# Scratch memory of a two-layer block laid out by pairs of heads: half the loads per group of the RWKV scan, the keys' rows in two buffers

## The chip, the cores and the metric

The kernel runs on one core of one Trainium2 chip. The metric is the device time of one launch in microseconds (us), the median of several runs. A core has TensorE (PE for its matmuls, PEld for its weight loads), VectorE (DVE), ScalarE (ACT), GpSimd (POOL) and SyncE (SP), which issues nearly all DMAs here. Each engine runs its own instructions strictly in program order. A second name of an engine with a q (SPq, PEldq) is its sequencer, which issues and waits.

## The reference

Two layers over 1024 latent tokens (D = 1024) and 256 context tokens. The first mixes by pooling and a short convolution; the second runs a bidirectional RWKV-7 scan of 8 heads of width 64 beside a convolution branch, and projects both out. What the change touches is the scan and what feeds it:

```python
def wkv_scan(r, w, k, v, a, bb, s0, reverse):
    def step(s, inp):
        r_t, w_t, k_t, v_t, a_t, b_t = inp
        sa = jnp.einsum("bhvk,bhk->bhv", s, a_t)
        s = s * w_t[:, :, None, :] + sa[..., None] * b_t[:, :, None, :] + v_t[..., None] * k_t[:, :, None, :]
        return s, jnp.einsum("bhvk,bhk->bhv", s, r_t)
...
def rwkv_branch(...):
    kk = heads(k * k_k).astype(jnp.float32)
    kk = kk / jnp.maximum(jnp.sqrt(jnp.sum(kk * kk, axis=-1, keepdims=True)), 1e-12)
    for d in range(2):
        a = jax.nn.sigmoid(a0[d] + (ua @ a1[d]) @ a2[d])
        k_d = heads(k * (1.0 + (a - 1.0) * k_a)).astype(jnp.float32)
        s_fin, o = wkv_scan(r_h, heads(decay), k_d, v_h, -kk, kk * a_h, init, reverse=(d == 1))
```

So for each head and direction the scan needs rows `a` = -kk and `r` (queries), rows `b` = kk*a and `k` (keys), and the values `v`. The context is scanned first and its final state starts the scan of the tokens.

## The kernel before, in words

**Stages.** The first layer runs to about 600 us, `odd_in` (projections of the second layer, and the preparation of the scan's rows) to about 925 us, `scan` to the end. `odd_in` and `scan` are written as small generators. A planner, class `Lists`, runs them against a table of costs: `yield "P", 700` says that the code up to the next yield takes 700 ns of TensorE, `"S", 4800, 300` that it takes 4800 ns of SP's queue and that its data is there 300 ns later, `"R", "bk"` that a buffer of pool `bk` is needed. The planner's choice, made when the program is built, fixes the order of instructions on each engine; the chip then runs these orders and waits by semaphores alone. A changed cost or count of buffers (`RES`) therefore moves instructions on all engines.

**odd_in.** The 8 heads are 4 pairs j (128 partitions: two heads of 64), the 1280 tokens are 5 units u of 256 (u = 4 is the context). `prep(j, u)` makes for both directions d and the 4 chunks of 64 tokens the query rows `ar` (slot 0: a, made on VectorE at L1247 and L1248; slot 1: r, made on GpSimd at L1240) and the key rows `bk` (L1222, L1223, L1244), and stores them to scratch memory in DRAM: `store_ar` to `ARD`, `turned` to `BKD` and, transposed, to `BTD`, `values` the transposed values to `VTD` (L1289).

**scan.** There are 20 groups G: two pairs of heads at a time (j and j+1, index c), 5 units, half a unit f (two chunks per direction). For each group:
- `group(G)` loads the query rows `w` from `ARD` (L1498, 8 loads: direction, head of the pair, pair), the key rows `bk` from `BKD` (L1505, 2 loads), and multiplies them on TensorE into scores `sc` (L1522), first for pair j, then for j+1. `w` has 5 buffers, `bk` has one.
- `invert(G)` gathers blocks of the scores (`eb`), stores them to `ED` (L1571, 2 DMAs), reads them back spread over partitions as `Bc` (L1578, 2 loads), and GpSimd inverts 16x16 triangular blocks in 15 steps (L1420, L1421).
- `levels(G)` builds the inverse up to 64x64 on TensorE (L1616, L1624, L1635, L1651), after ScalarE has copied GpSimd's result into `Xe` (L1608).
- `chain()` carries the state through the group's two steps: TensorE L1741, L1746, L1765, VectorE and ScalarE between. It needs the values `sv` (`load_sv`, L1670, 8 loads from `VTD`) and `bkt` (L1682, 2 loads from `BTD`).
- Beside it run matmuls of the convolution branch (`project`, L1960) and then of the output projection (L2102, L2307), placed by the planner in the gaps, and the convolution itself on VectorE (L1981).

**DMAs.** SP issues them one after the other. Each one uses one of eight semaphores in turn (DMAHW0 to DMAHW7), and waits before it is issued for the DMA that used the same semaphore before it, that is the one eight places earlier.

Of the kernel before, what the change touches and what calls it, by code (L numbers as in the profile page):

```python
# [179 lines left out]
class Kern:  # L180
# [727 lines left out]
    def odd_in(self, es):  # L908
# [247 lines left out]
        def prep(j, u):  # L1156
# [65 lines left out]
            nc.vector.tensor_tensor(out=bk[:, 0, :, 0, :], in0=c4(ta[:, 0, :]), in1=fold(F, 0, 0), op=ALU.mult)  # L1222
# [8 lines left out]
            ar = sp.tile([128, 2, 2, 4, 64], F32, tag="ar", name="ar")  # L1231

            def ends():
# [3 lines left out]
                if u < 4:  # L1237
                    yield "E", ("shift", j, 2)
                    yield "G", 1230
                    nc.gpsimd.tensor_tensor(out=ar[:, :, 1], in0=c4(rT[:, z]).unsqueeze(1).to_broadcast([128, 2, 4, 64]), in1=folds(E), op=ALU.mult)  # L1240
# [6 lines left out]
            nc.vector.scalar_tensor_tensor(out=ar[:, 0, 0], in0=c4(kk2), scalar=-2.0, in1=fold(E, 0, -1), op0=ALU.mult, op1=ALU.mult)  # L1247
            nc.vector.scalar_tensor_tensor(out=ar[:, 1, 0, :, ::-1], in0=c4(kk2), scalar=-2.0, in1=fold(E, 1, 1), op0=ALU.mult, op1=ALU.mult)  # L1248
# [27 lines left out]
        def values(j, u, v):  # L1276
# [12 lines left out]
            nc.sync.dma_start(out=self.VTD[j, u].rearrange("f p v -> p f v"), in_=Vx)  # L1289
# [1133 lines left out]
```

## Time and profile before

| | |
|---|---|
| median of 3 runs | 1552.14 us (1549.43 to 1553.41) |
| the profiled execution | 1545.31 us, its span 1543.5 us |
| TensorE busy, weight loads busy | 1381.1 us (89%), 1084.7 us (70%) |
| VectorE, ScalarE, GpSimd busy | 993.9 us (64%), 637.0 us (41%), 671.9 us (44%) |
| mean granted TensorE clock | 0.951 |
| chain that ended last | TensorE 49%, VectorE 17%, DMA 11%, GpSimd 10% |
| DMA | 174374 packets, 232.32 MB, 151 GB/s mean |

In a row of groups the fields are: line, engine, operation, out<-in, shapes, count, then busy us and mean ns of one, then the idle time of the engine ahead of it and what ended it. A row of waits reads: who waited for whom, us in total, times, the longest. A row of windows gives the stretch, its length, the busy us (and instructions) of PE, PEld, DVE, ACT and POOL, the granted clock, the DMA engines' share and GB/s. A row of the time line gives start, us, engine, line, operation; SPq rows are the issuing of DMAs.

### The profile page before, as it was taken

What the parts mean: (1) busy time and instruction counts of PE and PEld (TensorE: products, weight loads), DVE (VectorE), ACT (ScalarE), POOL (GpSimd) and SP (SyncE); (2) the same over time, 40 slices, a digit from 0 to 9 for tenths busy, and PEclk for the clock granted to TensorE, in tenths of its full rate; (3) what the DMA queues carried; (4) which work ended last, traced back from release to release, by engine and by line L of the source; (5) the groups of instructions that cost most, each with busy time, mean ns of one, the idle gap of its engine ahead of it and who ended that gap; (6) DMA issues with size and microseconds to landing.
All of it is one profiled execution on the core that took longest, in us unless ns stands there. A gap on an engine that the chain in (4) does not pass through costs nothing.

```text
span 1543.5 us, 32203 instructions
## 1 busy us (share of the span) xinstructions
PE 1381.1 (89%) x12820; PEld 1084.7 (70%) x12820; DVE 993.9 (64%) x1681; ACT 637.0 (41%) x1257; POOL 671.9 (44%) x925
## 2 busy tenths in 40 slices
PE   6899999998999999899889878888998988886996
PEld 1578788887888778677667656676776666764775
DVE  3744464545822561279999964778688777788567
ACT  2551112122322552356556531344445643657534
POOL 1343535548455532135545421755557246406003
PEclk9899999999999999999999989899998998898999
DMA  7413433634253210537657775655655566774223
GB/s 266 152 66 123 169 131 129 213 137 162 70 174 124 67 65 33 147 99 218 199 169 226 224 253 150 159 141 150 168 141 151 165 157 173 218 225 127 86 86 109
DMA packets 174374, 232.32 MB, mean 151 GB/s; under 512 B 38832, under 2 KB 130352, under 8 KB 174096
## 3 DMA queue, kind: packets, MB, share of 16 engines
q1 hardware_dynamic: 172928, 228.69, 48.7%
q8 instruction: 101, 1.65, 0.5%
q10 hardware_dynamic: 1296, 1.57, 0.3%
q14 instruction: 49, 0.40, 0.1%
HBM read 164.93 MB, written 63.31 MB: 148 GB/s over the span
## 4 chain that ended last, share of the span: by engine, by line
PE 49%; DVE 17%; DMA 11%; POOL 10%; issue 6%; ACT 5%; SPq 2%; DVEq 0%; POOLq 0%; ACTq 0%
PE d L302 25%; PE d L2102 3%; PE d L1960 3%; PE d L1016 3%; DMA Bc<-ED 2%; POOL X L1421 2%; POOL tmp L1420 2%; DMA bk<-BKD 2%; PE sc L1522 2%; PE d L944 2%; DMA ad<-in_ada_e 1%; POOL wl L268 1%; PE pa L1741 1%; PE pr L458 1%; DVE Z L1090 1%
## 5 line engine op out<-in xcount | busy, mean ns | idle before, releaser
L302 PE MATMUL d<-sx,wh 128*128 128x512 f32 x1152 | 365.8, 399 | 2.4 <-DVE sx L528 1.3
L302 PEld LDWEIGHTS d<-sx,wh 128*128 128x128 f32 x1152 | 220.5, 192 | 54.2 <-POOL sx L398 1.8
L302 PE MATMUL d<-sx,wl 128*128 128x512 f32 x576 | 233.1, 405 | 12.3 <-POOL wl L268 9.1
L1420 POOL TENSOR_TENSOR tmp<-X,Bc 128x120 f32<-128x120 f32 (+2 forms) x300 | 120.0, 400 | 195.0 <-DMA Bc<-ED 172.6
L1016 PE MATMUL d<-sx,wh 128*128 128x512 f32 x512 | 162.8, 400 | 0.0
L268 POOL TENSOR_TENSOR wl<-wr,wh 128x1024 fp32r<-128x1024 f32 x37 | 98.8, 2671 | 139.4 <-ACT wh L267 139.4
L629 DVE SCALAR_TENSOR_TENSOR junk<-wra,cb 128x1024 bf16<-128x1024 f32 x56 | 108.3, 1934 | 75.5 <-DMA wra<-in_ada_o 51.0
L1960 PE MATMUL d<-sx,wh 128*128 128x512 f32 x384 | 139.3, 430 | 0.0
L302 PEld LDWEIGHTS d<-sx,wl 128*128 128x128 f32 x576 | 110.4, 192 | 38.7 <-POOL wl L268 10.1
L1421 POOL TENSOR_TENSOR X<-X,tmp 128x120 f32<-128x120 f32 (+2 forms) x300 | 124.8, 416 | 23.5
L1016 PEld LDWEIGHTS d<-sx,wh 128*128 128x128 f32 x512 | 98.6, 193 | 22.1 <-issue 2.7
L1016 PE MATMUL d<-sx,wl 128*128 128x512 f32 x256 | 112.9, 441 | 0.0
L302 PE MATMUL d<-sc,wh 128*128 128x256 f32 x576 | 104.1, 281 | 0.0
L1960 PE MATMUL d<-sx,wl 128*128 128x512 f32 x192 | 83.8, 437 | 9.8 <-DVE wl L1934 9.8
L1981 DVE SCALAR_TENSOR_TENSOR acc<-hc,vec,acc 128x960 f32<-128x960 f32 (+14 forms) x120 | 90.0, 774 | 1.1
L302 PEld LDWEIGHTS d<-sc,wh 128*128 128x128 f32 x576 | 88.8, 190 | 1.4
L267 ACT CAST wh<-wr 128x1024 fp32r<-128x1024 f32 x37 | 38.7, 1046 | 119.8 <-PE d L302 64.5
L1960 PEld LDWEIGHTS d<-sx,wh 128*128 128x128 f32 x384 | 74.5, 200 | 16.5 <-issue 0.2
L302 PE MATMUL d<-sc,wl 128*128 128x256 f32 x288 | 81.0, 281 | 0.0
L1522 PE MATMUL sc<-w,bk 64*128 64x128 f32 (+1 forms) x640 | 55.4, 311 | 20.4 <-issue 9.1
L1522 PEld LDWEIGHTS sc<-w,bk 64*128 64x128 f32 x640 | 46.8, 210 | 28.2 <-issue 25.2
L1536 DVE TENSOR_TENSOR w<-sc,cstb 64x256 f32<-64x256 f32 x80 | 33.8, 422 | 47.2 <-PE sc L1522 28.5
(381 smaller groups left out, 2880.6 us busy)
## 6 DMA issues: line engine op xcount, KB each, us to landing
wr<-in_in_o SPq DMA_DIRECT2D x32, 512.0 KB
wr<-in_in_e SPq DMA_DIRECT2D x24, 512.0 KB
wra<-in_ada_o SPq DMA_DIRECT2D x24, 512.0 KB
BKD<-bk SPq DMA_DIRECT2D x40, 256.0 KB
BTD<-X SPq DMA_DIRECT2D x20, 512.0 KB
bk<-BKD SPq DMA_DIRECT2D x40, 256.0 KB
Bc<-ED SPq DMA_DIRECT2D x20, 512.0 KB
bkt<-BTD SPq DMA_DIRECT2D x40, 256.0 KB
```

Source lines behind the costliest of these rows:

```text
L267: self.nc.scalar.copy(hi, raw)
L268: self.nc.gpsimd.tensor_tensor(out=lo, in0=raw, in1=hi.bitcast(F32), op=ALU.subtract)
L302: self.nc.tensor.matmul(ps[:, :n], lhsT=w[a][:, k, :], rhs=rhs(src, k, b, c0, n), start=(i == 0), stop=(i == len(seq) - 1))
L629: nc.vector.scalar_tensor_tensor(out=junk, in0=w, scalar=1.0, in1=cb[:, s, :], op0=ALU.mult, op1=ALU.mult, accum_out=dst[:, s:s + 1])
L1016: nc.tensor.matmul(ps, lhsT=w[a][:, k, :], rhs=rhs(s, k, b, c0, m), start=(q == 0), stop=(q == len(seq) - 1))
L1420: g.tensor_tensor(out=t, in0=X[:, :, j:j + 1].to_broadcast([128, 8, m]), in1=B[:, j, :, j + 1:16] if j < 8 else B2[:, j - 8, :, j - 7:8], ...
L1421: g.tensor_tensor(out=X[:, :, j + 1:16], in0=X[:, :, j + 1:16], in1=t, op=ALU.add)
L1522: nc.tensor.matmul(ps[h][:, d, i, h:h + 1] if ctx else ps[h][:, d, i], lhsT=bk[R[h], c, d, i], rhs=w[R[h], c, d, sl, i, :], start=True, st ...
L1536: nc.vector.tensor_tensor(out=w[o, c, :, 2 * h], in0=ps[h][o, :, :, h], in1=ma[o].unsqueeze(2).to_broadcast([64, 2, 2, 64]), op=ALU.mult)
L1960: nc.tensor.matmul(ps, lhsT=wt(a, k), rhs=rhs("x", k, b, c0, 512), start=(i == 0), stop=(i == len(seq) - 1))
L1981: nc.vector.scalar_tensor_tensor(out=acc[:, o], in0=hc[:, q], scalar=w, in1=acc[:, o], op0=ALU.mult, op1=ALU.add)
L2102: nc.tensor.matmul(ps, lhsT=wt(a, at), rhs=ysrc(k, b, c0), start=(i == 0), stop=(i == len(seq) - 1))
```

## The change

`ARD` is laid out with the half unit f ahead of the direction, and `VTD` with chunk beside value, so that what a group needs of one direction and one head is one contiguous run for each row (1 KB of query rows in place of two of 512 B, 512 B of values in place of two of 256 B), and one DMA brings it for both pairs: `w` takes 4 loads in place of 8, `sv` 4 in place of 8. To write these layouts, the r rows on GpSimd are made in two instructions in place of one, the upper half of `ar` is stored in runs of 512 B in place of 1 KB, and the values in two stores of 256 B runs in place of one of 512 B runs. The factors -2 and 0.5 move between the instructions on VectorE (`ka`, `bk`, `ar`), whose count stays. The pool `bk` of the scan has two buffers; the tile `new` of the chain goes, `old` is updated in place. The planner's costs of SP for `w`, `sv`, `bk`, `ED`, `Bc` and the stored values change with it.

```diff
-    RES = dict(w3=[0.0] * 5, bk=[0.0], e=[0.0] * 3, ...
+    RES = dict(w3=[0.0] * 5, bk=[0.0] * 2, e=[0.0] * 3, ...
...
-        nc.vector.tensor_scalar(out=ka[:, 8:12], in0=self.vcol("k_k", 0, 4), scalar1=0.5, scalar2=None, op0=ALU.mult)
+        nc.vector.tensor_scalar(out=ka[:, 8:12], in0=self.vcol("k_k", 0, 4), scalar1=-1.0, scalar2=None, op0=ALU.mult)
...
-        self.ARD = dr.tile([NJ, 5, 128, 2, 2, 256], F32, name="ARD")
+        self.ARD = dr.tile([NJ, 5, 128, 2, 2, 2, 128], F32, name="ARD")
-        self.VTD = dr.tile([NJ, 5, 2, 128, 128], F32, name="VTD")
+        self.VTD = dr.tile([NJ, 5, 2, 2, 64, 2, 64], F32, name="VTD")
...
+        def fold2(t, d, sh):
+            return bass.AP(tensor=t.tensor, offset=t[:, d, 1 + sh:2 + sh].offset, ap=[list(t.ap[0]), [130, 2], [65, 2], [1, 64]])
...
-            nc.vector.tensor_tensor(out=bk[:, 0, :, 0, :], in0=c4(ta[:, 0, :]), in1=fold(F, 0, 0), op=ALU.mult)
+            nc.vector.scalar_tensor_tensor(out=bk[:, 0, :, 0, :], in0=c4(ta[:, 0, :]), scalar=-0.5, in1=fold(F, 0, 0), op0=ALU.mult, op1=ALU.mult)
...
-                    yield "G", 1230
-                    nc.gpsimd.tensor_tensor(out=ar[:, :, 1], in0=c4(rT[:, z]).unsqueeze(1).to_broadcast([128, 2, 4, 64]), in1=folds(E), op=ALU.mult)
+                    yield "G", 1600
+                    for d in range(2):
+                        nc.gpsimd.tensor_tensor(out=ar[:, :, d, 1], in0=c22(rT[:, z]), in1=fold2(E, d, 0), op=ALU.mult)
...
-            nc.vector.scalar_tensor_tensor(out=ar[:, 0, 0], in0=c4(kk2), scalar=-2.0, in1=fold(E, 0, -1), op0=ALU.mult, op1=ALU.mult)
+            nc.vector.tensor_tensor(out=ar[:, :, 0, 0], in0=c22(kk2), in1=fold2(E, 0, -1), op=ALU.mult)
...
-            yield "S", 600, 2500
-            nc.sync.dma_start(out=self.VTD[j, u].rearrange("f p v -> p f v"), in_=Vx)
+            yield "S", 1200, 2500
+            for c in range(2):
+                nc.sync.dma_start(out=self.VTD[j, u, :, :, :, c].rearrange("f h s v -> s (f h) v"),
+                                  in_=Vx[64 * c:64 * c + 64].rearrange("s f (h v) -> s (f h) v", h=2))
...
-            yield "S", 4800, 300
+            yield "S", 2400, 2500
             for d in range(2):
-                u, o = UN[d][g], 128 * side(d, f)
                 for h in range(2):
-                    for c in range(2):
-                        a = slice(2 * h, 2 * h + 1) if ctx else slice(h, h + 2)
-                        b = slice(h, h + 1) if ctx else slice(0, 2)
-                        nc.sync.dma_start(out=w[R[h], c, d, a].rearrange("p s c t -> p s (c t)"), in_=self.ARD[j + c, u, R[h], d, b, o:o + 128])
+                    b, sl = (slice(h, h + 1), slice(2 * h, 2 * h + 1)) if ctx else (slice(0, 2), slice(h, h + 2))
+                    nc.sync.dma_start(out=w[R[h], :, d, sl].rearrange("p c s i t -> p c (s i t)"),
+                                      in_=self.ARD[j:j + 2, UN[d][g], R[h], side(d, f), d, b].rearrange("c p s t -> p c (s t)"))
...
-            yield "S", 1200, 2900
+            yield "S", 1200, 3000
...
-            yield "S", 1200, 2400
+            yield "S", 1200, 3000
...
-            yield "S", 1200, 3600
+            yield "S", 1200, 4500
...
-                yield "S", 4800, 2200
+                yield "S", 2400, 2500
                 for h in range(2):
                     for d in range(2):
-                        for c in range(2):
-                            nc.sync.dma_start(out=sv[h][R[1 - h], c, d],
-                                              in_=self.VTD[j + c, UN[d][g], side(d, f), :, 64 * h:64 * h + 64].rearrange("(c s) v -> s c v", s=64))
+                        nc.sync.dma_start(out=sv[h][R[1 - h], :, d].rearrange("p c i v -> p c (i v)"),
+                                          in_=self.VTD[j:j + 2, UN[d][g], side(d, f), h].rearrange("a s c v -> s a (c v)"))
...
-                            nc.vector.tensor_tensor(out=new, in0=pa[:, :, 1], in1=old, op=ALU.add)
+                            nc.vector.tensor_tensor(out=old, in0=pa[:, :, 1], in1=old, op=ALU.add)
```

The rows below are the built order of instructions; a row's number of lines is that of the program it is from (in the changed kernel the loads of `w`, `bk`, `ED`, `Bc`, `sv`, `bkt` are L1507, L1515, L1581, L1588, L1679, L1691, the scores L1532 and the branch's matmuls L1968), and xN counts equal ones in a row.

SP at the start of the scan, from its first load on, before:

```order
L1498 DMA w_7354<-ARD 64x128 x8
L294 DMA wr<-in_in_o 128x1024
L1505 DMA bk<-BKD 128x2x256 x2
L1498 DMA w_7355<-ARD 64x128 x8
L1498 DMA w_7356<-ARD 64x2x128 x8
L1571 DMA ED_7334<-eb 128x128
L1571 DMA ED_7335<-eb 128x64
L1505 DMA bk<-BKD 128x2x256 x2
L294 DMA wr<-in_in_o 128x1024
L1498 DMA w_7357<-ARD 64x2x128 x8
L1578 DMA Bc<-ED_7334 128x1x1024
```

and in the changed kernel:

```order
L1507 DMA w_7389<-ARD 64x2x128 x4
L1507 DMA w_7390<-ARD 64x2x128 x4
L294 DMA wr<-in_in_o 128x1024
L1515 DMA bk<-BKD 128x2x256 x2
L1507 DMA w_7391<-ARD 64x2x256 x4
L1515 DMA bk<-BKD 128x2x256 x2
L1507 DMA w_7392<-ARD 64x2x256 x4
L1507 DMA w_7393<-ARD 64x2x256 x4
L1515 DMA bk<-BKD 128x2x256 x2
L1581 DMA ED_7370<-eb 128x128
L1581 DMA ED_7371<-eb 128x64
```

The second group's keys (the second `bk` row) stood behind 29 DMAs of the scan and now stand behind 15; the third group's now stand ahead of the first `ED`.

SP in one turn of the loop in mid-scan, from the load of one group's `w` to the next, before:

```order
L1498 DMA w_8949<-ARD 64x2x128 x8
L2023 DMA ZSD<-z 128x1024
L294 DMA wr<-in_in_o 128x1024
L1571 DMA ED_7336<-eb 128x128
L1571 DMA ED_7337<-eb 128x64
L1670 DMA sv_8950<-VTD 64x2x64 x4
L1670 DMA sv_8951<-VTD 64x2x64 x4
L1578 DMA Bc<-ED_7336 128x1x1024
L1578 DMA Bc<-ED_7337 128x1x512
L1505 DMA bk<-BKD 128x2x256 x2
L1682 DMA bkt<-BTD 128x2x256 x2
L1498 DMA w_9243<-ARD 64x2x128 x8
```

and in the changed kernel:

```order
L1507 DMA w_8959<-ARD 64x2x256 x4
L294 DMA wr<-in_in_o 128x1024
L1588 DMA Bc<-ED_7372 128x1x1024
L1588 DMA Bc<-ED_7373 128x1x512
L1679 DMA sv_8960<-VTD 64x2x128 x2
L1679 DMA sv_8961<-VTD 64x2x128 x2
L1515 DMA bk<-BKD 128x2x256 x2
L1691 DMA bkt<-BTD 128x2x256 x2
L1581 DMA ED_7370<-eb 128x128
L1581 DMA ED_7371<-eb 128x64
L1507 DMA w_9295<-ARD 64x2x256 x4
```

A group's 24 loads and stores are now 16; `Bc` stands ahead of `sv` here, and `bk` still directly behind both.

TensorE at the first two groups, the last scores of the first group and what follows, before:

```order
L1522 MATMUL sc_7443<-w_7354,bk 128x64
L1522 MATMUL sc_7444<-w_7354,bk 128x64
L1960 MATMUL d<-sx_128,wh 128x512
L1960 MATMUL d<-sx_127,wh 128x512
L1960 MATMUL d<-sx_129,wl 128x512
L1960 MATMUL d<-sx_130,wh 128x512
L1960 MATMUL d<-sx_129,wh 128x512
L1960 MATMUL d<-sx_131,wl 128x512
L1960 MATMUL d<-sx_132,wh 128x512
L1960 MATMUL d<-sx_131,wh 128x512
L1960 MATMUL d<-sx_117,wl 128x512
L1960 MATMUL d<-sx_118,wh 128x512
```

and in the changed kernel:

```order
L1532 MATMUL sc_7482<-w_7389,bk 128x64
L1532 MATMUL sc_7483<-w_7389,bk 128x64
L1968 MATMUL d<-sx_128,wh 128x512
L1968 MATMUL d<-sx_127,wh 128x512
L1968 MATMUL d<-sx_129,wl 128x512
L1968 MATMUL d<-sx_130,wh 128x512
L1968 MATMUL d<-sx_129,wh 128x512
L1968 MATMUL d<-sx_131,wl 128x512
L1968 MATMUL d<-sx_132,wh 128x512
L1968 MATMUL d<-sx_131,wh 128x512
L1532 MATMUL sc_7512<-w_7390,bk 128x64
L1532 MATMUL sc_7513<-w_7390,bk 128x64
```

The second group's scores come 8 branch matmuls after the first group's, before it was 36. Counted over the whole scan in such matmuls ahead of them, the last step of the chain stands behind 576 of L1960 and 120 of L2102, before behind 576 and 135.

More of the change, by code (lines that the diff above doesn't have):

```diff
@@ L192 @@
     LAT = dict(P=300, A=300, D=300, G=300, S=2000)
-    RES = dict(w3=[0.0] * 5, bk=[0.0], e=[0.0] * 3, rr=[0.0] * 4, sc=[0.0], eb=[0.0], Bc=[0.0] * 2, X=[0.0], lv=[0.0], qt=[0.0] * 3,
+    RES = dict(w3=[0.0] * 5, bk=[0.0] * 2, e=[0.0] * 3, rr=[0.0] * 4, sc=[0.0], eb=[0.0], Bc=[0.0] * 2, X=[0.0], lv=[0.0], qt=[0.0] * 3,
                bkt=[0.0] * 3, sv=[0.0] * 3, psd=[0.0] * 2, z=[0.0], hc=[0.0] * 2, acc=[0.0], post=[0.0] * 2,
@@ L1104, in fold, with c22 @@
             return bass.AP(tensor=t.tensor, offset=t[:, d, 1 + sh:2 + sh].offset, ap=[list(t.ap[0]), [65, 4], [1, 64]])
+        def c22(ap):
+            return ap.rearrange("p (f c t) -> p f c t", f=2, t=64)
+        def fold2(t, d, sh):
+            return bass.AP(tensor=t.tensor, offset=t[:, d, 1 + sh:2 + sh].offset, ap=[list(t.ap[0]), [130, 2], [65, 2], [1, 64]])
         def folds(t):
@@ L1230, in prep @@
             yield "R", "ar"
-            ar = sp.tile([128, 2, 2, 4, 64], F32, tag="ar", name="ar")
+            ar = sp.tile([128, 2, 2, 2, 2, 64], F32, tag="ar", name="ar")
             def ends():
@@ L1246, in prep @@
             yield "D", 670
-            nc.vector.scalar_tensor_tensor(out=ar[:, 0, 0], in0=c4(kk2), scalar=-2.0, in1=fold(E, 0, -1), op0=ALU.mult, op1=ALU.mult)
-            nc.vector.scalar_tensor_tensor(out=ar[:, 1, 0, :, ::-1], in0=c4(kk2), scalar=-2.0, in1=fold(E, 1, 1), op0=ALU.mult, op1=ALU.mult)
+            nc.vector.tensor_tensor(out=ar[:, :, 0, 0], in0=c22(kk2), in1=fold2(E, 0, -1), op=ALU.mult)
+            nc.vector.tensor_tensor(out=ar[:, :, 1, 0, :, ::-1], in0=c22(kk2), in1=fold2(E, 1, 1), op=ALU.mult)
             js = [spawn(store_ar(j, u, ar, je), pr)]
@@ L1295, in store_ar @@
             if u < 4:
-                nc.sync.dma_start(out=self.ARD[j, u, 0:64].rearrange("p d s t -> p (d s t)"), in_=ar[0:64].rearrange("p d s c t -> p (d s c t)"))
+                nc.sync.dma_start(out=self.ARD[j, u, 0:64].rearrange("p f d s t -> p (f d s t)"), in_=ar[0:64].rearrange("p f d s c t -> p (f d s c t)"))
                 for sl in range(2):
-                    nc.sync.dma_start(out=self.ARD[j, u, 64:128, :, 1 - sl, :], in_=ar[64:128, :, sl].rearrange("p d c t -> p d (c t)"))
+                    nc.sync.dma_start(out=self.ARD[j, u, 64:128, :, :, 1 - sl, :].rearrange("p f d t -> p (f d) t"),
+                                      in_=ar[64:128, :, :, sl].rearrange("p f d c t -> p (f d) (c t)"))
             else:
@@ L1301, in store_ar @@
                     r = slice(64 * h, 64 * h + 64)
-                    nc.sync.dma_start(out=self.ARD[j, u, r, :, h, :], in_=ar[r, :, 0].rearrange("p d c t -> p d (c t)"))
+                    nc.sync.dma_start(out=self.ARD[j, u, r, :, :, h, :].rearrange("p f d t -> p (f d) t"),
+                                      in_=ar[r, :, :, 0].rearrange("p f d c t -> p (f d) (c t)"))
             free("ar")
@@ L1694, in chain @@
             old = gp.tile([128, 2, 2, 64], F32, name="old")
-            new = gp.tile([128, 2, 2, 64], F32, name="new")
             rh = gp.tile([128, 2, 2, 64], F32, name="rh")
@@ L1774, in chain @@
                         for h in C2:
-                            nc.vector.tensor_tensor(out=both(nx, h, cn), in0=pa[R[h], :, 1] if first else new[R[h]], in1=decay(h), op=ALU.mult)
+                            nc.vector.tensor_tensor(out=both(nx, h, cn), in0=pa[R[h], :, 1] if first else old[R[h]], in1=decay(h), op=ALU.mult)
                     if jo:
@@ L2410 @@
     from concourse.bass_utils import run_bass_kernel_spmd
-    nc = bacc.Bacc("TRN2", target_bir_lowering=False, num_devices=1, dynamic_dma_scratch_size=1024)
+    nc = bacc.Bacc("TRN2", target_bir_lowering=False, num_devices=1, dynamic_dma_scratch_size=256)
     arrays = _layout({k: np.asarray(v) for k, v in inputs.items()})
```

2 lines of the change are left out of this document (1 added, 1 removed).

## The prediction

> **What bounds the kernel now.** I first read the busy time by stretch, to see where TensorE, the busiest engine, stands still: `odd_in` from 625, the scan from 925, the output projection mostly from 1400 us on.
>
> ```profile
> 625.00:925.00 300.00, 262.47 (x1465) 206.94 (x1464) 245.91 (x339) 160.21 (x275) 120.81 (x132) 0.96 0.64 196
> 925.00:1400.00 475.00, 408.60 (x7404) 316.37 (x7402) 351.62 (x767) 216.03 (x529) 235.63 (x583) 0.92 0.61 164
> ```
>
> The second row is the stage that the change is about. PE is busy for 408.60 of 475.00 us, so 66.4 us are idle, and the clock granted is 0.92. The clock has a price of its own: if it is either full or half, 0.92 means half for 16% of 475 us, 76 us, and work that fits into 38 us at full clock takes that long. So 66.4 us of idle time stand beside about 38 us lost to the clock, 0.57 us for each idle us. That this hangs together is read at two stops, the stretch of idle PE and then what follows:
>
> ```profile
> 1218.20:1220.40 2.20, 0.04 (x2) 0.04 (x1) 2.02 (x7) 0.59 (x3) 1.81 (x6) 0.99 0.91 254
> 1220.40:1223.80 3.40, 3.40 (x33) 3.06 (x34) 0.95 (x3) 1.12 (x3) 1.97 (x9) 0.50 1.04 368
> ...
> 1240.50:1244.40 3.90, 0.01 (x1) 0.00 (x0) 1.74 (x4) 2.19 (x6) 2.70 (x6) 0.98 1.11 237
> 1244.40:1247.80 3.40, 3.36 (x38) 3.05 (x40) 0.32 (x1) 0.73 (x2) 2.77 (x9) 0.52 0.75 196
> 1247.80:1260.00 12.20, 12.14 (x182) 9.47 (x180) 11.35 (x28) 6.00 (x16) 7.12 (x18) 1.00 0.50 131
> ```
>
> After 2.2 and after 3.9 us of idle PE the clock is 0.50 and 0.52 for 3.4 us, then full again: a stop costs its length and about 1.7 us more. The Trainium skill, "TensorE: Matmul & The Clock Gate" (HAM oscillation), sets the bound at idle gaps of about 3.4 us; the first stop, of 2.2 us, was already enough here, so the row decides, and I charge every idle us of this stage at 1.57.
>
> Next, what PE waits for in this stretch (rows of PE's matmuls; their weight loads wait at the same time):
>
> ```profile
> PE PI L1616 <- ACT Xe L1608: 10.2, 3, 5.7
> PE sc L1522 <- issue: 9.1, 4, 4.1
> PE sc L1522 <- DMA bk<-BKD: 8.9, 5, 3.9
> PE pa L1765 <- ACT sv L1751: 6.3, 5, 3.8
> PE PI L1624 <- issue: 5.4, 3, 2.8
> PE pa L1746 <- DVE rh L1743: 4.1, 6, 1.4
> PE pa L1741 <- DVE sv L1775: 3.6, 5, 2.3
> ```
>
> The scores (L1522) lead with 9.1 + 8.9 = 18.0 us. "Issue" names no releaser, but the stop at 1240.5 shows what it is, in the time line of SP's queue and PE there:
>
> ```profile
> 1227.63 5.62 SPq L1670 DMA_DIRECT2D sv<-VTD  x8
> ...
> 1234.00 1.27 SPq L1578 DMA_DIRECT2D Bc<-ED  x2
> 1235.36 2.48 SPq L1505 DMA_DIRECT2D bk<-BKD  x2
> ...
> 1241.24 8.71 SPq L1498 DMA_DIRECT2D w<-ARD  x8
> ...
> 1244.44 2.17 PE L1522 MATMUL sc<-w,bk 64*128 64x128 f32 x16 [3.92 <-DMA bk<-BKD]
> ```
>
> The keys are issued only at 1235.36, since SP was at the values and at `Bc` until then, and land 9 us later behind `Bc`'s 768 KB. With one buffer they could not have been asked for before the scores of the group ahead had ended, and then they stand in SP's row. That row has no gaps in mid-scan:
>
> ```profile
> 1021.08 1.05 SPq L1505 DMA_DIRECT2D bk<-BKD  x2
> 1022.23 0.89 SPq L1571 DMA_DIRECT2D ED<-eb  x2
> 1023.16 0.97 SPq L1682 DMA_DIRECT2D bkt<-BTD  x2
> 1024.18 0.47 SPq L1984 DMA_DIRECT2D CVD<-acc  x1
> 1024.74 6.68 SPq L1498 DMA_DIRECT2D w<-ARD  x8
> 1031.52 1.25 SPq L1578 DMA_DIRECT2D Bc<-ED  x2
> 1032.88 8.14 SPq L1670 DMA_DIRECT2D sv<-VTD  x8
> 1041.07 1.11 SPq L1682 DMA_DIRECT2D bkt<-BTD  x2
> ```
>
> From 1021.08 to 1042.18 SP issues without a stop, one group long; of 21 us `w` and `sv` take 6.68 + 8.14 = 14.8. Last, the chain that ended last, taken over the scan alone:
>
> ```profile
> by line: PE d L1960 10.7%; DMA Bc<-ED 8.1%; POOL X L1421 8.0%; POOL tmp L1420 7.5%; DMA bk<-BKD 7.5%; PE sc L1522 6.4%; issue 5.8%; PE pa L1741 2.8%; PE pa L1746 2.3%; PE pa L1765 2.2%; PE po L1736 1.8%; DVE eb L1566 1.5%; DMA wr<-in_in_o 1
> ```
>
> Two loads that wait in that row, `bk` with 7.5% of 475 us (36 us) and `Bc` with 8.1% (38 us), are on it. So the scan is held by a late SP queue, at PE's price for stops.
>
> **The change, part by part.**
>
> *Half the loads of `w` and `sv`.* Durations of one issue (min/median/max):
>
> ```profile
> L1498 SPq DMA_DIRECT2D w<-ARD x160: 445/599/1722, 923.1 to 1338.2; - x160
> L1670 SPq DMA_DIRECT2D sv<-VTD x160: 573/605/2022, 962.7 to 1372.0; - x160
> ```
>
> 80 of each go. The new loads move twice the bytes in as many runs (64 partitions, two runs each), so I keep the median: 80 x 0.599 + 80 x 0.605 = 96 us of SP's row less, 4.8 us of some 21 in each group. For PE this is worth only what its lateness costs there. With `bk` in two buffers, asked for a group (some 20 us) ahead, a landing of 9 us is covered, and I take the whole 18.0 us of the scores' wait: 18.0 x 1.57 = 28.3 us (bounds: nothing, and all that PE waits for a load or for what hangs on `Bc`, below).
>
> The Trainium skill, "DMA: Bandwidth & Descriptors" (Issuing engines are not separate DMA queues), says that the sequencer's time to initiate a DMA "is usually small relative to the DMA itself"; by it the 96 us would be worth nothing and the sum would be about zero. The row without gaps speaks against it here; what it would make of the time is the second rival.
>
> *`Bc` earlier.* PE's 10.2 us at L1616 and 5.4 at L1624 come at the end of eb, `ED`, `Bc`, GpSimd, `Xe`. The change takes 2.4 us of `w` from ahead of `Bc`, but not `Bc`'s own landing, nor GpSimd's 15 steps. I take half of the 10.2: 5.1 x 1.57 = 8.0 us (bounds: 0, and 15.6 x 1.57 = 24.5).
>
> *What is late next.* When the groups come closer, the chain itself is: its steps wait 6.3 + 4.1 + 3.6 = 14.0 us now, for ScalarE and VectorE, and VectorE is busy for 351.62 of 475 us. I let these waits double: +14.0 (bounds 0 and 28).
>
> *`odd_in`.* The rows that the change touches, and who on PE waits for GpSimd's next one:
>
> ```profile
> L1240 POOL TENSOR_TENSOR ar<-Z,E 128x512 f32<-128x512 f32 x16 | 21.7, 1356 | 0.4 <-DMA ARD<-ar 0.4
> L1256 POOL TENSOR_TENSOR kb<-kd 128x256 f32<-128x256 f32 x16 | 15.9, 996 | 19.3 <-DMA BON<-kb 15.2 <-DVE thw L1197 3.7 <-DVE ar L1248 0.3
> L1222 DVE TENSOR_TENSOR bk<-ta,F 128x256 f32<-128x256 f32 x20 | 15.6, 780 | 1.2 <-PE w L1173 0.3 <-DMA BKD<-bk 0.2 <-ACT Vx L1286 0.2
> L1247 DVE SCALAR_TENSOR_TENSOR ar<-kkm,E 128x256 f32<-128x256 f32 x20 | 15.4, 768 | 0.2 <-DMA ARD<-ar 0.2
> ...
> L1289 SPq DMA_DIRECT2D VTD<-Vx x20: 359/371/677, 684.9 to 883.7; - x20
> ...
> PE m L1265 <- DVE kb L1260: 7.0, 6, 3.0
> ```
>
> The r rows in two instructions of 256 elements cost, by the row of `kb`, 2 x 996 against 1356 ns: 0.64 us more in each of 16 units, at least nothing. `kb` stands behind them on GpSimd, then L1260 on VectorE, then PE's L1265, which waits 6 times now: 6 x 0.64 = 3.8 if each passes on. I take +3 (bounds 0 and 16 x 0.64 = 10). VectorE: the two forms cost alike (780 and 768 ns), zero, in an engine's row that keeps its count. 20 more stores of values are 20 x 0.371 = 7.4 us of SP, which issues in `odd_in` with room between; their 256 B runs go where nobody waits before the scan: zero. The chain's sum in place and the planner's numbers issue nothing; their effect is the order, above.
>
> Sum: -28.3 - 8.0 + 14.0 + 3 = -19.3 us, against the profiled execution's own 1545.31 (span 1543.5 and 1.8 around it): 1526. The median of the runs, 1552.14, lies 6.8 above that execution; less 19.3 it is 1533.
>
> **The rivals.** *All that hangs on loads goes* (0.12): scores and inversion no longer make PE wait and the chain keeps up, (18.0 + 10.2 + 5.4) x 1.57 = 52.8 us, 1499. For it: `Bc` and `bk` share one row and both come earlier. Against: `Bc` still lands some 7 to 9 us after its issue, and that DMA share of 0.61 hardly falls, since no byte less is moved.
>
> *No change* (0.14): transfers, not their issue, are late. SP's row is full because each DMA waits for the one eight places before it, and `Bc` is slow to land; its rows of waits are
>
> ```profile
> SPq L1498 <- DMA Bc<-ED: 30.0, 19, 2.6
> ...
> SPq L1670 <- DMA Bc<-ED: 11.5, 8, 2.7
> ```
>
> 41.5 us in which SP only waited for `Bc`. With 8 loads less to a group the eighth behind a `Bc` is reached sooner, and SP waits longer there for what it no longer issues. Then scores come as late as now: 1552, within 4.7 us (0.3%, about what runs of this kernel can tell apart). Against: the stop at 1240 is behind `sv`, and the second buffer asks for the keys a group ahead in any case.
>
> *Slower* (0.18): the new order on TensorE asks too early. It sets scores and steps further ahead in the branch's matmuls (8 in place of 36 ahead of the second group's, at the end 120 in place of 135), while `Bc` lands as now and GpSimd needs as long; PE, in order, then stops at L1616 in groups where it doesn't now. One stop there costs 10.2 / 3 = 3.4 us, with the clock 5.3. The gain of 36.3 is eaten by 7 such stops more; with the 14.0 and 3 as above 4 are enough to be even, and with 8 of the 17 groups that don't stop now the sum is -19.3 + 42.7 = +23, 1575. For it: GpSimd has 172.6 us of waits for `Bc` already. Against: the costs that the order was made with rise for `ED` and `Bc` (2400 to 3000, 3600 to 4500), which places what follows later.
>
> ```profile
> POOL tmp L1420 <- DMA Bc<-ED: 172.6, 14, 36.4
> ```
>
> **How the numbers follow.** The sum, with its bounds in ordinary combinations, covers 1518 to 1546: 0.56. The larger gain 0.12, no change 0.14, slower 0.18. The sum's range ends at the edge of "no change", so faster by over 0.3% is 0.56 + 0.12 = 0.68, within 0.3% 0.14, slower 0.18. The predicted time is the sum's, 1533. The range for 8 in 10 runs from 1505 (about half of the larger gain) to 1560 (the lower part of the slower case, one to two stops past break-even): what lies outside is 0.06 below and 0.12 above. The likeliest case alone: 1518 to 1546.
>
> **What the profile after would show.** If right: the loads of `w` and `sv` 80 each at some 0.6 us, gaps in SP's row in mid-scan; the scores' waits on PE between 925 and 1400 us down from 18.0 to under 5; half-clock stretches fewer, the granted clock of that stretch above 0.92; PE's idle time there below 50 us; waits at L1741, L1746, L1765 above 14. `odd_in` as long as now within 5 us. Wrong would be the first step if the issue of one new load took about 1.2 us, the second if PE waited at L1616 for more than 25 us, the third if the chain's waits passed 30, and all of it if PE's stops moved with the new order to places where nothing waits now, which the time line of each engine would show as new releasers.

## The result and the profile after

The changed kernel took 1520.88 us (median of 4 runs, 1514.42 to 1530.60), the kernel before beside it 1550.79 (1547.48 to 1553.41): ratio 0.9828, 95% interval 0.9801 to 0.9855, so about 27 us or 1.7% faster (the two medians lie 30 us apart). Forecast were 1533 and a gain of 19. The profiled execution of after is the slowest of its four, 1530.60 us (span 1528.8); against the profiled one of before (1545.31) it is only 14.7 us shorter. The times of after spread by 1%, those of before by 0.4%. So the kernel was timed and profiled again, unedited:

> The changed kernel once more, unedited, in five rounds, since its first four runs spread by 1% and the profiled one was the slowest of them. If the first comparison (0.9828) stands, 1516 to 1526, and the version with three loads of Bc (0.9755) is really the faster by some 10 us. If the changed kernel's median is below 1514, the three loads are worth nothing. The second profile also tells which of PE's waits of the first (7.1 us in one stop at L1626 among them) belong to the kernel and which to that one execution.

Measured: 1523.75 us (1520.17 to 1528.88), ratio 0.9827 (0.9791 to 0.9863); this profiled execution has a span of 1522.8. The first result stands, and below I use both profiles.

The busy time by stretch, first the rows of after, then the second profile's row for the scan alone (columns as in the prediction's first fence):

```profile
625.00:925.00 300.00, 262.38 (x1461) 206.82 (x1459) 247.07 (x337) 159.51 (x275) 128.97 (x148) 0.95 0.65 194
925.00:1400.00 475.00, 417.83 (x7769) 324.88 (x7770) 357.58 (x786) 227.35 (x555) 253.37 (x620) 0.92 0.63 169
```

```profile
925.00:1400.00 475.00, 417.94 (x7842) 323.88 (x7842) 362.13 (x796) 229.97 (x561) 255.21 (x620) 0.93 0.63 171
```

`odd_in` is as it was. In the scan's stretch PE issues 7769 matmuls where it issued 7404; it is idle for 57.2 us in place of 66.4, at a granted clock that is hardly higher (0.92, 0.93). From 5 us ahead of the first scores to PE's last instruction, PE's idle time (summed from the trace) fell from 82.0 to 69.0 us, and the time in which the clock stood at half from 99.0 to 90.3 us. The 13.0 us and half of the 8.7 make 17.3, and this stretch is 17.1 us shorter; it begins 2.2 us later, so the span lost 14.7. In the second profile the two are 68.5 and 75.6 us: 13.5 and half of 23.4 make 25.2, against a stretch shorter by 23.5 and a span shorter by 20.7.

SP's issues after (groups by line; min/median/max in ns):

```profile
L1507 SPq DMA_DIRECT2D w<-ARD x80: 573/605/2002, 925.4 to 1304.6; - x80
L1679 SPq DMA_DIRECT2D sv<-VTD x80: 573/598/1745, 944.3 to 1349.9; - x80
L1298 SPq DMA_DIRECT2D VTD<-Vx x40: 574/608/1385, 683.4 to 888.8; - x40
```

A load of twice the bytes takes SP as long as a load of half of them, so the 96 us of issuing are gone, as worked out. Over the whole scan's stretch (475 us, summed from the trace) SP's issues took 338 us before and take 233 after; its waits for engines rose from 62 to 179 us, those for earlier DMAs went from 77 to 68 (issues and waits overlap a little). The row that had no gaps has them now, in the same group as the prediction's fence (SP's time line, from this group's `ED` to the next one's; the us of a row with several DMAs hold the waits between them too, so only 4 x 0.6 = 2.4 of the 6.48 us of `sv` are issuing):

```profile
1022.86 0.81 SPq L1581 DMA_DIRECT2D ED<-eb  x2
1025.70 1.32 SPq L1588 DMA_DIRECT2D Bc<-ED  x2
1027.12 2.56 SPq L1507 DMA_DIRECT2D w<-ARD  x4
1029.77 6.48 SPq L1679 DMA_DIRECT2D sv<-VTD  x4
1036.29 1.12 SPq L1691 DMA_DIRECT2D bkt<-BTD  x2
1037.45 1.83 SPq L1515 DMA_DIRECT2D bk<-BKD  x2
1046.20 0.81 SPq L1581 DMA_DIRECT2D ED<-eb  x2
```

After the last load SP issues nothing from 1039.28 to 1046.20. And `Bc` goes out at 1025.70, 2.8 us after `ED`; before it went out at 1031.52, 9.3 us after `ED` at 1022.23, behind 6.68 us of `w`. What that means for GpSimd's first step, the row of before and then that of after:

```profile
1038.74 0.84 POOL L1420 TENSOR_TENSOR tmp<-X,Bc 128x120 f32<-128x120 f32 x1 [12.84 <-DMA Bc<-ED]
```

```profile
1032.93 0.40 POOL L1432 TENSOR_TENSOR tmp<-X,Bc 128x120 f32<-128x120 f32 x1 [6.49 <-DMA Bc<-ED]
```

Both start 7.2 us after `Bc`'s issue: the landing takes as long as before, the inversion begins 5.8 us earlier because SP asked earlier. Who waits after, on PE, GpSimd and SP's queue between 925 and 1400 us:

```profile
PE d L1968 <- DVE wl L1942: 9.7, 2, 8.4
PE PI L1626 <- ACT Xe L1618: 8.0, 2, 7.1
PE PI L1645 <- issue: 7.3, 3, 3.6
PE pa L1749 <- DVE sv L1783: 6.7, 7, 2.0
PE pa L1773 <- ACT sv L1759: 6.2, 4, 3.2
PE PI L1634 <- issue: 5.2, 4, 3.5
PE PI L1626 <- issue: 3.4, 2, 3.0
...
PE sc L1532 <- DMA bk<-BKD: 0.7, 2, 0.5
```

```profile
POOL tmp L1432 <- DMA Bc<-ED: 122.1, 13, 27.5
```

```profile
SPq L1581 <- DVE eb L1578: 64.3, 12, 13.0
SPq L1691 <- DMA Bc<-ED: 26.1, 11, 3.2
...
SPq L1679 <- DMA Bc<-ED: 16.1, 9, 2.2
```

Of the first row's 9.7 us, 8.4 are one stop at the start of the scan that ends at 925.9 us, just inside this stretch; before, the same stop (9.6 us) ended at 923.6, just outside. The scores' waits went from 18.0 to 0.7 us, GpSimd's for `Bc` from 172.6 to 122.1. SP now waits 64.3 us for VectorE's `eb`: it is early where it was late. It still waits 26.1 + 16.1 = 42.2 us in these two rows behind `Bc` for the semaphore eight places back (51.8 in all rows together, 41.8 in the second profile, 49.2 before), but these waits now fall into a row with room. About half of what GpSimd no longer waits for `Bc` it waits elsewhere, before it fills `X`, for ScalarE's copy of the last group's `X`; the row of before and that of after:

```profile
POOL X L1416 <- ACT Xe L1608: 22.9, 18, 3.8
```

```profile
POOL X L1428 <- ACT Xe L1618: 48.6, 19, 5.6
```

The chain that ended last, over the same stretch, no longer lists `bk`:

```profile
by line: PE d L1968 17.8%; issue 7.2%; PE sc L1532 5.5%; DMA Bc<-ED 5.4%; POOL tmp L1432 5.3%; POOL X L1433 5.2%; PE pa L1749 3.6%; PE pa L1773 3.5%; PE pa L1754 3.2%; PE po L1744 2.7%; DMA ms<-BON 2.3%; DVE acc L1989 2.2%; PE po L1767 2.2%
```

The second profile's chain has no `bk` among its larger shares either, but `Bc` has 8.7% there and GpSimd's two lines 9.2 and 8.4%, no less than before: the way through `Bc` and GpSimd is still on it.

### The profile page after: what moved, and what is told of

It reads as the page before. It is cut to its first block, busy times and chain, and to the rows that moved or that the text cites. A ratio compares the mean times of both kernels' runs of the same rounds, so it can differ in the third digit from the quotient of the medians.

```text
span 1528.8 us, 32066 instructions
## 1 busy us (share of the span) xinstructions
PE 1379.8 (90%) x12820; PEld 1084.3 (71%) x12820; DVE 998.1 (65%) x1681; ACT 640.1 (42%) x1259; POOL 682.4 (45%) x941
## 3 DMA queue, kind: packets, MB, share of 16 engines
q10 hardware_dynamic: 1296, 1.57, 0.3%
## 4 chain that ended last, share of the span: by engine, by line
PE 54%; DVE 17%; DMA 9%; POOL 8%; issue 7%; ACT 4%; SPq 2%; DVEq 0%; ACTq 0%; POOLq 0%
PE d L302 24%; PE d L1968 6%; PE d L1016 5%; PE d L2110 3%; PE sc L1532 2%; DMA Bc<-ED 2%; POOL tmp L1432 2%; PE d L944 2%; POOL X L1433 2%; POOL wl L268 1%; PE pa L1749 1%; PE pa L1773 1%; PE pa L1754 1%; PE d L2315 1%; DMA ad<-in_ada_e 1%
## 5 line engine op out<-in xcount | busy, mean ns | idle before, releaser
L1432 POOL TENSOR_TENSOR tmp<-X,Bc 128x120 f32<-128x120 f32 (+2 forms) x300 | 121.2, 404 | 144.6 <-DMA Bc<-ED 122.1
L629 DVE SCALAR_TENSOR_TENSOR junk<-wra,cb 128x1024 bf16<-128x1024 f32 x56 | 112.9, 2016 | 74.5 <-DMA wra<-in_ada_o 50.0
L1968 PE MATMUL d<-sx,wh 128*128 128x512 f32 x384 | 139.0, 432 | 0.0
L302 PEld LDWEIGHTS d<-sx,wl 128*128 128x128 f32 x576 | 110.6, 192 | 38.3 <-POOL wl L268 9.9
L1433 POOL TENSOR_TENSOR X<-X,tmp 128x120 f32<-128x120 f32 (+2 forms) x300 | 125.7, 419 | 23.5
L1968 PE MATMUL d<-sx,wl 128*128 128x512 f32 x192 | 83.3, 434 | 9.7 <-DVE wl L1942 9.7
L1968 PEld LDWEIGHTS d<-sx,wh 128*128 128x128 f32 x384 | 74.4, 201 | 16.3
L1222 POOL TENSOR_TENSOR kd<-kd,Z 128x512 f32<-128x512 f32 x20 | 29.6, 1482 | 77.4 <-DVE kd L1218 77.4
L647 POOL TENSOR_TENSOR lraw<-lraw,lhi 128x1024 fp32r<-128x1024 f32 x15 | 38.4, 2558 | 48.2 <-ACT lhi L646 48.2
L1016 PEld LDWEIGHTS d<-sx,wl 128*128 128x128 f32 x256 | 49.3, 193 | 11.3 <-issue 1.9
```

What stands on the lines that cost most here:

```text
L302: self.nc.tensor.matmul(ps[:, :n], lhsT=w[a][:, k, :], rhs=rhs(src, k, b, c0, n), start=(i == 0), stop=(i == len(seq) - 1))
L629: nc.vector.scalar_tensor_tensor(out=junk, in0=w, scalar=1.0, in1=cb[:, s, :], op0=ALU.mult, op1=ALU.mult, accum_out=dst[:, s:s + 1])
L647: nc.gpsimd.tensor_tensor(out=raw.bitcast(F32R), in0=raw, in1=hi.bitcast(F32), op=ALU.subtract)
L1016: nc.tensor.matmul(ps, lhsT=w[a][:, k, :], rhs=rhs(s, k, b, c0, m), start=(q == 0), stop=(q == len(seq) - 1))
L1432: g.tensor_tensor(out=t, in0=X[:, :, j:j + 1].to_broadcast([128, 8, m]), in1=B[:, j, :, j + 1:16] if j < 8 else B2[:, j - 8, :, j - 7:8], ...
L1433: g.tensor_tensor(out=X[:, :, j + 1:16], in0=X[:, :, j + 1:16], in1=t, op=ALU.add)
```

## The experiments

The theory to be tested, Q: SP's row of issues is what is late, and half the loads free it. Its rivals: B, that the second buffer of `bk` carries the gain (the prediction's reason for taking the scores' whole wait); and O, that the new order does. Each ratio is to the kernel before, run beside it.

**Buffer, order, loads.** First, the changed kernel with one buffer of `bk`:

```diff
-    RES = dict(w3=[0.0] * 5, bk=[0.0] * 2, ...
+    RES = dict(w3=[0.0] * 5, bk=[0.0], ...
```

> The changed kernel with one buffer of bk in place of two; the planner orders the instructions anew for it. If the second buffer carries the gain (the keys asked for a group ahead), PE waits at the scores again (18 us or so between 925 and 1400) and the time goes back to 1540 to 1550. If the halved number of loads carries it (SP's row has room, so the keys are issued as soon as their buffer is free), it stays within 8 us of the changed kernel, 1521 to 1529.

Measured: 1520.52 us, ratio 0.981 (0.9763 to 0.9858), the same as after. The scores wait again a little (one stop of 6.9 us), but nothing comes of it:

```profile
PE pa L1754 <- DVE rh L1751: 12.8, 10, 3.7
...
PE sc L1532 <- DMA bk<-BKD: 7.6, 2, 6.9
```

Then the other side of it, the kernel before with a second buffer of `bk` (with `old` updated in place and the smaller DMA scratch area that the changed kernel has too, to make room):

```diff
-    RES = dict(w3=[0.0] * 5, bk=[0.0], ...
+    RES = dict(w3=[0.0] * 5, bk=[0.0] * 2, ...
...
-                            nc.vector.tensor_tensor(out=new, in0=pa[:, :, 1], in1=old, op=ALU.add)
+                            nc.vector.tensor_tensor(out=old, in0=pa[:, :, 1], in1=old, op=ALU.add)
```

> The kernel before with two buffers of bk and nothing else (the chain's sum is made in place to leave room); old layout, 8 + 8 loads, old costs, the planner's order for two buffers. If the second buffer is what the scores lacked, 10 to 20 us of the 30 are here: 1530 to 1540. If SP's row is what is late, the keys are asked for earlier but everything else stands behind them in a full row: 1545 to 1555.

Measured: 1549.81 us, ratio 1.0012 (0.9982 to 1.0042): no change. The rows say why:

```profile
PE PI L1616 <- ACT Xe L1608: 24.0, 9, 7.1
...
PE sc L1522 <- DVE rr L1541: 1.6, 3, 1.1
```

The scores' 18.0 us are gone and PE stops at the inversion's first product instead, 9 times and 24.0 us where it was 3 times and 10.2. The wait that I had counted as the gain only moved to what is late next. B falls, with one reservation: the count of buffers also moves the planner's order, so these two runs are not the buffer alone.

Now loads and order apart: the changed layout with 4 + 4 loads and one buffer, but with the planner's costs of before, so that the order is like before's (shown: `w`, `Bc`, `sv`; `bk` and `ED` likewise; in its trace each group's scores stand behind as many branch matmuls as before, plus 16):

```diff
-            yield "S", 2400, 2500
+            yield "S", 4800, 300
...
-            yield "S", 1200, 4500
+            yield "S", 1200, 3600
...
-                yield "S", 2400, 2500
+                yield "S", 4800, 2200
```

> The changed layout and the 4 + 4 loads of w and sv per group, but with the planner's old costs of SP and one buffer of bk, so that the scan's order on TensorE and VectorE is that of before. If fewer issues on SP are the cause by themselves (theory of the queue), most of the gain of 30 us is here: 1522 to 1532. If the new order is the cause, it is not: 1540 to 1553.

and the changed kernel's order with 8 + 8 loads, two for each one of after:

```diff
-                    nc.sync.dma_start(out=w[R[h], :, d, sl].rearrange("p c s i t -> p c (s i t)"),
-                                      in_=self.ARD[j:j + 2, UN[d][g], R[h], side(d, f), d, b].rearrange("c p s t -> p c (s t)"))
+                    for c in range(2):
+                        nc.sync.dma_start(out=w[R[h], c, d, sl].rearrange("p s i t -> p (s i t)"),
+                                          in_=self.ARD[j + c, UN[d][g], R[h], side(d, f), d, b].rearrange("p s t -> p (s t)"))
```

(and `sv` likewise).

> The changed kernel with its own order on all engines, but w and sv fetched pair by pair again, 8 + 8 loads per group in runs of 1 KB and 512 B, placed where the 4 + 4 stand. Theory of the queue: 96 us of issuing come back into SP's row, and in an order that counts on half of it PE stops more than before: 1545 to 1570. Theory of the order: SP's issues cost little, 1521 to 1530.

Measured, with the kernels before and after at the corners (ratio to before):

| | 8 + 8 loads a group | 4 + 4 loads |
|---|---|---|
| order of before | 1 (before) | 0.9875 (0.9812 to 0.9937), 1531.45 us |
| order of after | 1.0166 (1.0121 to 1.0212), 1575.99 us | 0.9828 (0.9801 to 0.9855) |

In the old order the halved loads alone give about 19 us. The new order gives some 7 more with few loads (the intervals overlap), and costs 26 us with many (6 us above what even Q had expected): it counts on a row that has room. O alone would have made the kernel slower. (The kernel before has its old layout; the other three have the new one, whose share no run separates.) One stop outside the scan changes with the order: near 1400 us, at the start of the output projection, PE waits 8.6 us for VectorE's `wl` before, 8.3 with 4 + 4 loads in the old order, and 1.7 in both profiles of after. Whether the 7 us are this stop no run tells. In the new order the 160 issues are worth 0.0338 x 1550 = 52 us. With 8 + 8 loads the scores wait for `bk` as before, and others with them:

```profile
PE pa L1751 <- DVE sv L1785: 11.2, 6, 6.7
PE PI L1627 <- ACT Xe L1619: 10.5, 2, 10.2
...
PE sc L1533 <- DMA bk<-BKD: 10.1, 5, 5.2
```

**Which of the loads.** The same edit for `sv` alone, and for `w` alone:

> The changed kernel with its order and layout, but the values sv fetched in 8 loads a group in place of 4 (80 issues more, some 48 us of SP's row); w stays in 4. With both in 8 loads the time was 1576 against 1521. If each issue in SP's row costs alike, half of the 55 us comes back: about 1548 (1540 to 1556). If it is w that matters (it feeds the scores, and the values have slack), about 1525 to 1532. If the values hold the chain, 1560 or more.

> The changed kernel with its order and layout, but the query rows w fetched in 8 loads a group in place of 4 (80 issues more, some 46 us of SP's row); sv stays in 4. If each issue costs alike: about 1548 (1540 to 1556), the same as with sv in 8. If w is what matters: 1560 or more, with waits of the scores back. If w, which has 5 buffers and is asked for early, has slack: 1525 to 1532.

Measured: 1546.82 us, 0.9982 (0.9962 to 1.0002), and 1545.05 us, 0.9978 (0.9951 to 1.0004). Against the 0.9828 of after that is 24 and 23 us, together 47 of the 52. Query rows, asked for early into five buffers, and values, which the chain needs at once, cost the same: it is their place in SP's row that costs, not who reads them. Nor do more DMAs make `Bc` land later: its way from its issue to GpSimd's first step is 8.1 us with 8 + 8 loads and 8.3 and 8.9 in the two profiles after (table below). 80 issues of 0.6 us are 48 us of SP and half of that in time. This bears on the Trainium skill, "DMA: Bandwidth & Descriptors" (Issuing engines are not separate DMA queues), by which the sequencer's time to initiate a DMA is usually small relative to the DMA: not so here, where after and the three kernels with 8 loads of one or both move the same bytes. The granted clock tells the same, in the scan's row of each (`sv` in 8 loads, then `w`):

```profile
925.00:1400.00 475.00, 410.43 (x7648) 318.17 (x7648) 340.77 (x752) 217.83 (x532) 232.85 (x590) 0.90 0.59 163
```

```profile
925.00:1400.00 475.00, 411.57 (x7680) 318.74 (x7680) 347.21 (x761) 219.97 (x536) 237.88 (x591) 0.89 0.59 165
```

**Where the lateness acts.** From the traces I took, for the 20 groups, the path from the end of VectorE's gather (`eb`) to GpSimd's last step, in us (means; the single group shown above is one of the twenty):

| kernel | `eb` to `ED` | `ED` to `Bc`, issue to issue | `Bc`'s issue to first step | 15 steps | whole path | ratio to before |
|---|---|---|---|---|---|---|
| before | 2.4 | 7.1 | 8.0 | 14.5 | 32.0 | 1 |
| before, two `bk` | 3.3 | 6.6 | 8.0 | 14.2 | 32.1 | 1.0012 |
| after, 8 + 8 loads | 3.7 | 6.0 | 8.1 | 14.1 | 31.9 | 1.0166 |
| after, `w` in 8 | 1.8 | 4.9 | 8.5 | 14.5 | 29.6 | 0.9978 |
| after, `sv` in 8 | 1.9 | 5.1 | 8.0 | 14.1 | 29.2 | 0.9982 |
| 4 + 4 loads, old order | 0.4 | 5.4 | 9.2 | 14.8 | 29.8 | 0.9875 |
| after, second profile | 0.9 | 4.1 | 8.9 | 14.7 | 28.6 | 0.9827 |
| after | 0.9 | 3.9 | 8.3 | 14.6 | 27.7 | 0.9828 |
| after, one `bk` | 0.3 | 4.3 | 8.6 | 14.5 | 27.6 | 0.981 |

The change shortens this path by 4.3 us a group (3.4 in the second profile), all of it in SP's row (2.4 + 7.1 becomes 0.9 + 3.9); `Bc`'s way to the first step and GpSimd's steps do not get shorter. Theory P says that this path sets the pace of the scan. Three groups of runs try it. First, the planner told that `Bc` lands later:

```diff
-            yield "S", 1200, 4500
+            yield "S", 1200, 7000
```

> The changed kernel, the planner's latency of the load Bc raised from 4500 to 7000 ns, nearer to the landing of 7 to 10 us that the traces show; no instruction more or less, another order. If PE's stops at the inversion's products (L1626, L1634, L1645, some 24 us after the change) come from asking before Bc can be there, they fall below 12 us and the time to about 1505 to 1512. If Bc and GpSimd are simply as fast as the groups follow each other, the stop moves to another place and the time stays within 1516 to 1526.

Measured: 1529.64 us, 0.9845 (0.9788 to 0.9901), the path 28.1. No gain (3.6 us above the upper band): PE's stops at L1626, L1634 and L1645 do not come from a wrong number in the plan that a better one would mend. Second, one `Bc` of 1 MB:

```diff
-            for t, b in zip(ED[G % 2], (eb, eb2)):
+            for t, b in zip(ED[G % 2], (eb,)):
...
-            for i, (t, b) in enumerate(zip(ED[G % 2], (B, B2))):
-                n = 8 * t.shape[2]
-                nc.sync.dma_start(out=b.rearrange("p k x -> p (k x)"),
-                                  in_=t.rearrange("q i c -> q (i c)")[:, i * n:i * n + n].unsqueeze(1).to_broadcast([8, 16, n]))
+            nc.sync.dma_start(out=B.rearrange("p k x -> p (k x)"),
+                              in_=ED[G % 2][0].rearrange("q i c -> q (i c)").unsqueeze(1).to_broadcast([8, 16, 2048]))
```

> The changed kernel with one buffer of bk, and the gathered blocks stored once and read back by one load of 128 x 2048 (1 MB) in place of two of 128 x 1024 and 128 x 512 (768 KB): 2 issues less per group, 40 in all, some 20 us of SP's row, and one copy on VectorE less, for a third more bytes of Bc. If SP's row is still what holds the scan, as fewer issues of w and sv would have it: about 1508 to 1516. If the landing of Bc counts from here on, its 256 KB more make it slower: 1528 to 1540.

Measured: 1604.87 us, 1.0344 (1.0316 to 1.0372), 83 us slower than after with one `bk` and far outside what either side had expected. GpSimd's first step needs the first load only; that was 512 KB and is now 1 MB, and it starts 13.9 us after the issue (median) in place of 7.6. `Bc`'s issue to first step is 14.3 in the mean, the path 33.2 us. GpSimd's waits for `Bc` are 174.5 us (104.4 in after with one `bk`), and the DMA behind `Bc` in SP's row pays too:

```profile
POOL tmp L1432 <- DMA Bc<-ED: 174.5, 17, 36.0
```

```profile
SPq L1674 <- DMA Bc<-ED: 67.1, 10, 9.2
```

```profile
925.00:1400.00 475.00, 384.80 (x6878) 300.10 (x6879) 302.36 (x653) 182.95 (x459) 226.66 (x578) 0.84 0.67 159
```

Two issues a group less were a loss, because what lands on the path counts more than the issue: 5.6 us of path in each of 20 groups cost 83 us. (SP's longer waits behind `Bc`, 92.5 us in all rows against 42.1, are in that figure, and I have not separated them.) Third, the opposite: the first load made smaller, by a third load, and by another place of the division.

```diff
-            for i, (t, b) in enumerate(zip(ED[G % 2], (B, B2))):
-                n = 8 * t.shape[2]
+            for t, b, lo, hi in ((ED[G % 2][0], B[:, 0:4], 0, 4), (ED[G % 2][0], B[:, 4:8], 4, 8), (ED[G % 2][1], B2, 8, 16)):
+                n = t.shape[2]
...
-                                  in_=t.rearrange("q i c -> q (i c)")[:, i * n:i * n + n].unsqueeze(1).to_broadcast([8, 16, n]))
+                                  in_=t.rearrange("q i c -> q (i c)")[:, lo * n:hi * n].unsqueeze(1).to_broadcast([8, 16, (hi - lo) * n]))
```

> The changed kernel, in the same order, with Bc brought by three loads (rows 0 to 3, 4 to 7, 8 to 15 of each block: 256 KB each) in place of two (512 and 256 KB): 20 issues more, the same bytes. GpSimd's first step needs the first load only, so it should start about 3.3 us earlier in each group (8.3 us after the issue becomes about 5). If the path from the gathered blocks to the inverse sets the pace of the scan (32.0 us a group before, 27.7 after, 33.2 in the version with one load of 1 MB, whose 6 us more cost 84 us), each us of it is worth 7 to 15 us of time: 1475 to 1505, with some 6 us against it for the issues. If it does so no longer at 27.7 us, because GpSimd's 15 steps, the chain or TensorE itself hold the groups apart, the 20 issues are all that is left: 1521 to 1530.

> Three loads of Bc as in the version with two buffers of bk, here with one buffer. With the buffer worth nothing, as measured before, the same time as that version within 6 us: 1475 to 1505 if the path to the inverse sets the pace, 1521 to 1530 if not. If the second buffer matters once groups follow more closely, this one is slower by 10 us or more, with the scores' waits for bk back above 10 us.

> The changed kernel with one buffer of bk (1520.5 by itself), the two loads of Bc divided after row 6 in place of 8 (384 and 400 KB in place of 512 and 256), no issue more. GpSimd's first step starts about 1.7 us earlier in each group, its seventh should find its rows there. If the path to the inverse sets the pace: 12 to 25 us less, 1495 to 1509. If not: 1516 to 1526.

| kernel | median us | ratio (interval) | `Bc`'s issue to first step, mean (median) | path |
|---|---|---|---|---|
| three loads, two `bk` | 1513.21 | 0.9755 (0.9727 to 0.9783) | 6.9 (6.8) | 26.5 |
| three loads, one `bk` | 1510.82 | 0.9755 (0.9717 to 0.9792) | 7.4 (7.3) | 26.5 |
| divided after row 6, one `bk` | 1514.86 | 0.9781 (0.9758 to 0.9805) | 8.5 (7.9) | 27.0 |

GpSimd waits less for `Bc` in the three-load versions, first with two buffers of `bk`, then with one:

```profile
POOL tmp L1432 <- DMA Bc<-ED: 97.5, 14, 27.4
```

```profile
POOL tmp L1432 <- DMA Bc<-ED: 76.7, 8, 26.7
```

Three loads with two buffers of `bk` are some 11 us faster than after (0.9755 against 0.9828, the intervals apart), the fastest kernels here. Both my bands (1475 to 1505, 1521 to 1530) missed it, and both bands for the division after row 6 missed too (1509, 1516). With one buffer of `bk` the three loads are as fast as with two. The size of the step was wrong: I had the first 256 KB land 3.3 us earlier, as their bytes would have it, and the first step starts 1.4 us earlier in the mean. The traces tell why, group by group. In the 13 groups where GpSimd waited for `Bc`, it began 5.6 us after the issue (median; 7.4 in after). In the other 7 the load was there, and GpSimd came later, behind ScalarE's copy of the last `X`; its waits there rose once more:

```profile
POOL X L1428 <- ACT Xe L1618: 64.7, 19, 8.0
```

So with a shorter landing what GpSimd waits for next is `X`, which has one buffer; no run gives it a second. The path is 1.2 us shorter in each group against the first profile of after and 2.1 against the second, so 5 to 9 us of time for each us of it, where the 1 MB load cost 15. With the division after row 6 GpSimd waited for `Bc` in only 8 groups (6.1 us after the issue, against 7.3 in 10 groups of after with one `bk`), so the mean first step hardly moved, and its ratio is not apart from that of after with one `bk`.

So P fits what was done to this path in the kernel after: longer by 5.6 us, 83 us slower (with SP's waits behind `Bc` in it); shorter by 1 to 2 us, 11 faster. It is not the whole: the kernel with 8 + 8 loads has the path of before and is 26 us slower, and 4 + 4 loads in the old order are faster than `sv` in 8 at about the same path. With a full row other things come late with it (scores, the chain's `sv`, above). How the 27 us of the change divide between the path and those, these runs don't settle.

## Why the prediction was right, and where not

The direction, its cause (SP's full row) and the range held; the gain of 19.3 us in the sum was 14.7 and 20.7 in the two profiled executions and 27 in the ratio of the runs. That the sum came so near is in part luck: its largest term stands for another cause than the one given, and the chain's term is more than twice too large.

- *Half the loads.* Right: 80 + 80 issues of 0.6 us, 96 us of SP gone, gaps in its row, and the time follows the number of issues (23 and 24 us for either 80). The row without gaps in the prediction was read too strongly: its 14.8 us of `w` and `sv` are 16 issues of 0.6 us, 9.7, and for the rest waits and a few longer issues, and of the 475 us before SP waited 62 for engines.
- *The scores' 18.0 us, taken whole at 1.57.* The wait went (0.7 and 1.2 us), as forecast. The reason given, the second buffer, was wrong: with one buffer the kernel is as fast. And the pricing was: the kernel before with two buffers loses the same wait and gains nothing, since PE stops at L1616 instead. A wait that vanishes is worth its length only if what is next in line is not late as well. That a gain came all the same is because the fewer issues made the next in line, `Bc`, earlier too; how much of the 28.3 that is, no run tells.
- *`Bc` earlier, -8.0.* Looked for in the wrong place. PE's waits at the product after `Xe`, 10.2 us at L1616, are 8.0 + 3.4 at L1626, and L1645 waits 7.3 more; all the inversion's products together wait for 22.1 us of the scan before, 27.3 and 23.0 in the two profiles after. But `Bc` is asked for 4.7 us (4.5 in the second profile) sooner after `eb` in each group, more than the 2.4 that I took; groups follow one another faster, and PE waits no less for the inversion at the quicker pace. The gain shows in GpSimd's waits (172.6 to 122.1) and not in PE's.
- *The chain's waits doubled, +14.0.* Mis-sized: with every row of them over the scan, the chain's steps wait 15.9 us before, 21.7 and 19.7 after: 4 to 6 more, not 14.
- *`odd_in`, +3.* Right in the mean: the branch's first matmul comes at 925.9, before at 923.6, 2.3 us later; in the twelve profiles with the new layout it comes between 922.4 and 928.4, 925.7 in the mean. PE's wait for `kb` is 9.8 us where it was 7.0. The stores of the values, put at nothing, take 0.608 us each, not the 0.371 of before, and are not quite free: ScalarE waits for them 6.1 us (3.2 before), and PE for ScalarE's `Vx` 5.2 (2.0 before).
- *The clock.* 0.57 us for each idle us was near: over the stretch used above, half of the half-clock time is 0.60 of the idle time before, 0.65 and 0.55 after. The granted clock above 0.92 came only in the second profile (0.93), PE's idle time below 50 us not at all (57).
- *The rivals.* "No change" had its wait right (SP behind `Bc` 51.8 and 41.8 us, about as long as the 49.2 before; the prediction's 41.5 lacks a third row, 7.7 us at `ED`) and its effect wrong: the row now has 179 us of waits for engines, and what was late in it is issued earlier. "Slower" had its mechanism right: the new order does ask early, at a price of 26 us if the loads stay many, and in the kernel before with two `bk` it is stops at the inversion's product that take the gained wait's place. "All that hangs on loads" was too much, since `Bc`'s way to the first step (8.0 us before, 8.3 and 8.9 after) and GpSimd's steps (14.5, 14.6 and 14.7) stay.
